# Second norm's transpositions placed at weight-tile boundaries of the out-projection, in a one-layer hybrid decoder trunk

## The chip, the core and the metric

The kernel runs on one core of a Trainium2 chip. The metric is the device time of one execution in microseconds (us); the median of several runs is compared. TensorE (PE) does the matrix work, VectorE (DVE), ScalarE (ACT) and GpSimd (POOL) the rest, SyncE (SP) issues most transfers.

## What is computed

One layer: RMSNorm, two token mixers merged by gates, an output projection added to the input, then a second RMSNorm and a squared-ReLU MLP added again, and a final norm. Sequence 1024, width 1024, MLP width 4096, float32. The part that matters here:

```
def rms_norm(x, gain):
    xf = x.astype(jnp.float32)
    y = xf * lax.rsqrt(jnp.mean(xf * xf, axis=-1, keepdims=True) + NORM_EPS)
    return (y * gain.astype(jnp.float32)).astype(x.dtype)
...
    y = jax.nn.sigmoid(m_a) * y_a + jax.nn.sigmoid(m_b) * y_b
    return y @ w_out
...
        h = rms_norm(x, norm_mix[l])
        x = x + hybrid_mixer(h, ...)
        h = rms_norm(x, norm_mlp[l])
        x = x + jnp.square(jax.nn.relu(h @ w_up[l])) @ w_down[l]
    return rms_norm(x, norm_final)
```

## The kernel before

**Matrix products.** Each float32 operand is split into a rounded high part and a rest (`split`: ACT casts the high part, DVE subtracts). `mm3` then issues three matmuls (lines 144, 145, 146 of the profile): high by high, high by rest, rest by high. Three matmuls of 128x512 into one PSUM bank are one step of a product.

**The out-projection, in two halves of 512 rows.** A row tile is 128 rows. `out_proj` does row tiles 0 to 3 of the sequence; its sums with the input land in `x2a`. The second half is written out in the loop over `part` (two parts of two row tiles each: 4 and 5, then 6 and 7) and `hf` (two halves of the 1024 output columns). Inside, `n` counts four steps, each with one weight tile `out_w[4 * hf + j]`, kept in SBUF: 2 k-slices x 2 row tiles x 3 matmuls = 12 matmuls. A part so has 96 matmuls. At the end of each `hf` DVE adds the sums to `x2s` (L1357). The last `hf` of part 1 takes its last two weight tiles first for one row tile, then for the other, so its `n` runs to 5.

**The second norm.** `second_norm(tt, half)` handles row tile `tt + 4 * half`. `norm_rows` squares and sums a row tile on ACT (L165), adds epsilon on DVE (L166), takes the power -0.5 on POOL (L171) and multiplies by it and the gain on DVE (L172, tile `xn_h`). Then eight 128x128 transpositions on TensorE (L1268) go into two banks of the PSUM tag "hg", which has two banks in all; ACT copies each bank back (L1269). For row tiles 0 to 3 the result is split at once into the operands B11 and B21. For 4 to 7 the generator `operands()` forms sums with row tile `tt` (t1, B22, n2, T3, T4: the operands of a seven-product Strassen scheme) and splits them.

**Behind it.** `product(q, step)` and `hidden(q, step)` are the up-projections of the MLP, by weight quads `q`. Three of their products (`uX` of quads 0 to 2) need only B11, one (`uZ`) B21; the others need the sums. `first_weights` and the calls after the loop prepare the split weights of quads 0 to 2 (`wA`, `ws10`, `ws30`, `wA120`) on ACT and DVE; they reuse SBUF tiles of weight tiles that the out-projection has finished with.

**What sets the order.** A scheduler orders each engine's instructions, within what the program pins. On TensorE `pin` keeps program order only while `pinned[0]` is true. Before the change this holds from `(part, hf) == (1, 1)` on; ahead of it the scheduler sets the transpositions of row tiles 0 to 5 among the matmuls of the parts. `keep` pins the norm's and the splits' operations on ACT and DVE.

Of the kernel before, what the change touches and what calls it, by code (L numbers as in the profile page):

```python
# [18 lines left out]
P = 128  # L19
# [26 lines left out]
def trunk(ctx: ExitStack, tc: tile.TileContext, x, wts, mlp, pv, gains, mask_f, mask_u, out):  # L46
    nc = tc.nc
    V, A, G, PE = nc.vector, nc.scalar, nc.gpsimd, nc.tensor
# [6 lines left out]
    def opened(name, **how):  # L55
        cm = tc.tile_pool(name=name, bufs=1, reuse_waits="tile", **how)
        return cm.__enter__(), lambda: cm.__exit__(None, None, None)
# [4 lines left out]
    def bank(tag, name):  # L62
        return ps.tile([P, 512], F32, tag=tag, name=name, bufs={"pj": 4, "sc": 2, "hg": 2}[tag])
# [3 lines left out]
    for i in range(NC * NPAIR):  # L67
        at = (0, 1, 2, 3, 4, 6, 5)
# [17 lines left out]
    def split(src, h, lo):  # L86
        keep(A.copy(h, src))  # L87
        ins = V.tensor_tensor(out=lo, in0=src, in1=h.bitcast(F32), op=ALU.subtract)  # L88
        keep(ins)
        return ins  # L90
# [45 lines left out]
    pinned = [False]  # L136

    def pin(ins):
        if pinned[0]:
            tc.keep_in_program_order(ins)  # L140

    def mm3(o, ah, al, bh, bl, first, last, goes_on=False):
        how = {"skip_group_check": True} if goes_on else {}
        pin(PE.matmul(o, ah, bh, start=first, stop=False, **how))  # L144
        pin(PE.matmul(o, ah, bl, start=False, stop=False, **how))  # L145
        pin(PE.matmul(o, al, bh, start=False, stop=last, **how))  # L146


    ident = const.tile([P, P], F32, tag="ident", name="ident")
# [668 lines left out]
    def stage(i):  # L818
        c, p = where(i)
        got = gots[i]  # L820
        if i == 0:
            yield from v_steps(c, p, got, lambda tt: None)
        elif i > 1:
            yield from v_of(i)

        def more(n):
            with tc.high_priority(400):
                transposed(xn1[n], hT[1], n, f"x1{n}")

        hooks = {at: lambda n=n: more(n) for at, n in {2: ((4, 1),), 3: ((2, 2), (6, 3))}.get(i, ())}  # L830
        px = yield from hooked(project_steps(c, f"xa{c}{p}"), hooks)
        xc, xps = conv_in(c, p, px)
        if i == 0:
            parameters()
            tc.keep_in_program_order(V.tensor_copy(mu, mu32.to_broadcast([P, 7, 8, 32])))
            pinned[0] = True
        yield
        if i == 1:
            gots[0]["tail"]()
            transposed(xn1[0], hT[1], 0, "x10")  # L840
        if i > 4:
            combos_on(2)

        def convolve():
            got["xc"] = conv(c, p, xc, xps, None)

        pq = yield from hooked(project_steps(c, f"q{c}{p}"), {} if i == 1 else {6: convolve})
        got["q1"] = q_of(c, p, pq)
        yield
        fs = hooked(project_steps(c, f"f{c}{p}"), {6: convolve} if i == 1 else {})  # L850
        for _ in range(5 if i != 1 else 7):
            next(fs)
            yield
        if i > 3:
            combos_on(1 if i == 4 else 2)
        if i == 1:
            pf = yield from fs
            got["f"], got["kk"] = f_of(c, p, pf)
            yield
        yield from rg_lru(c, p, got, *got["xc"])  # L860
        if i > 0:
            gots[i - 1]["normalised"]()
        for n in ((0,), (1,), (2, 3))[i] if i < 3 else ():
            xn1[n] = next_rows(n, gots[0]["states"] if i == 1 else None)
        if i != 1:
            pf = yield from fs
            got["f"], got["kk"] = f_of(c, p, pf)
# [74 lines left out]
    for i in range(NC * NPAIR):  # L942
        rest = stage(i + 1) if i + 1 < NC * NPAIR else last_stage()
# [238 lines left out]
    for q in own:  # L1182
        n = q + 1
# [60 lines left out]
    def homes(*names):  # L1244
        h2p.append(opened(f"h2{len(h2p)}", side="right"))
        for o in names:
            hop[o] = [h2p[-1][0].tile([P, 4, T], F32R, tag=o + q, name=f"h2{o}{q}") for q in ("H", "L")]
# [5 lines left out]
    def second_norm(tt, half):  # L1253
        cut = slice(tt * P, (tt + 1) * P)
        t = tt + 4 * half
        xs = x2s[tt] if half else x2a[tt]
        home = {3: "xn3", 4: "y01", 5: "y03", 6: "y00", 7: "y02"}.get(t, "xn")
        xn = n2p.tile([P, D], F32, tag=home, name=f"xn_h{t}", bufs=3 if home == "xn" else 1)
        norm_rows(xs, xn, gain1, f"h{t}")
        b = braw[tt, half] = xn.rearrange("p (h t) -> p h t", h=2)  # L1260

        def op_split(src, o):
            return split(src.rearrange("p (k t) -> p k t", k=4), hop[o][0][:, :, cut], hop[o][1][:, :, cut])

        for h in range(2):
            pt = bank("hg", f"xT_h{t}_{h}")
            for k in range(4):
                pin(PE.transpose(pt[:, k * P : (k + 1) * P], xn[:, (4 * h + k) * P : (4 * h + k + 1) * P], ident))  # L1268
            A.copy(b[:, h, :], pt)  # L1269
            if half == 0:  # L1270
                op_split(b[:, h, :], ("B11", "B21")[h])

        def operands():
            b0 = braw[tt, 0]
            b11, b21, b22, b12 = b0[:, 0, :], b0[:, 1, :], b[:, 1, :], b[:, 0, :]
            V.tensor_tensor(out=b11, in0=b11, in1=b12, op=ALU.subtract)
            t1_ops.append(op_split(b11, "t1"))
            yield
            for ins in (op_split(b22, "B22"), V.tensor_tensor(out=b12, in0=b22, in1=b12, op=ALU.subtract)):
                how = mybir.DependencyInfo(mybir.DependencyClass.NoSync, mybir.DependencyReason.DATA)  # L1280
                if tt > 1:
                    tc.add_manual_dep(ins.ins, t1_ops[-1].ins.name, how, reason="t1")
            V.scalar_tensor_tensor(b22, b11, -1.0, b22, op0=ALU.mult, op1=ALU.subtract)
            n2_ops.append(op_split(b22, "n2"))
            yield
            last = op_split(b12, "T3")
            if tt > 1:
                tc.add_manual_dep(last.ins, n2_ops[-1].ins.name, how, reason="n2")
            yield
            last = V.scalar_tensor_tensor(b21, b22, -1.0, b21, op0=ALU.mult, op1=ALU.subtract)  # L1290
            if tt > 1:
                tc.add_manual_dep(last.ins, n2_ops[-1].ins.name, how, reason="n2")
            op_split(b21, "T4")
            yield

        return operands()

    rest, t1_ops, n2_ops = [], [], []

# [26 lines left out]
                work[0]["sums"]()  # L1326
                work[0]["b"]()

    for tt in range(4):
        second_norm(tt, 0)  # L1330
    close_rows()
    homes("B22")
    for part in range(2):
        tts = (2 * part, 2 * part + 1)
        for tt in tts:
            x2s[tt] = n2p.tile([P, D], F32, tag="x2", name=f"x2s{tt}", bufs=2)
            nc.sync.dma_start(x2s[tt], x[(4 + tt) * P : (5 + tt) * P, :])
        for hf in range(2):
            pp = {tt: bank("pj", f"po1{hf}{tt}") for tt in tts}
            turn = [(j, tts) for j in range(4)]  # L1340
            if (part, hf) == (1, 1):
                turn = turn[:2] + [(j, tts[i : i + 1]) for i in range(2) for j in (2, 3)]
                pinned[0] = True
            for n, (j, those) in enumerate(turn):
                if n == 4:
                    first_weights()
                wh, wl = out_w[4 * hf + j]
                for k in range(2):
                    ku = 2 * j + k
                    yh, yl = ykt1(part, ku)  # L1350
                    cols = slice(k * 512, (k + 1) * 512)
                    for tt in those:
                        cut = slice((tt % 2) * P, (tt % 2 + 1) * P)
                        mm3(pp[tt], yh[:, cut], yl[:, cut], wh[:, cols], wl[:, cols], ku == 0, ku == 7)
            for tt in tts:
                cols = slice(hf * 512, (hf + 1) * 512)
                V.tensor_tensor(out=x2s[tt][:, cols], in0=pp[tt], in1=x2s[tt][:, cols], op=ALU.add)  # L1357
        for i, tt in enumerate(tts):
            if part:
                product(i, 0)  # L1360
            nc.sync.dma_start(x2d[4 + tt], x2s[tt])
            rest.append(second_norm(tt, 1))
    with tc.high_priority(400):
        work[0]["d"]()
    product(0, 3)
# [67 lines left out]
    for q in range(1, QUADS):  # L1433
        n = q + 1 if q + 1 < QUADS else QUADS + QUADS - 2
# [83 lines left out]
    for kb in range(n_kb):  # L1518
        last = kb + 1 == n_kb
        qs = order[2 * kb : 2 * kb + 2]  # L1520
        for half in range(2):
# [8 lines left out]
            for step, (bk, wo, uo), prs in [  # L1530
# [11 lines left out]
                for pr in prs:  # L1542
                    _, ci, cj, op = ADDS[step]
# [92 lines left out]
```

## Time and profile before

| | |
|---|---|
| runs, median (lowest to highest) | 1549.08 us (1548.0 to 1550.54), 3 runs |
| profiled execution: time, span | 1550.47 us, 1548.7 us |
| TensorE busy, matmuls | 1528.6 us, 9088 |
| DVE, ACT, POOL busy | 1151.0, 809.3, 154.5 us |
| mean granted TensorE clock | 0.999 |
| DMA | 306.82 MB, mean 198 GB/s |

The profile is of one execution; its times are us from the start of its span, the time from the first to the last instruction. In the timeline a row is: start, duration, engine, line, operation, output<-input, count, and in brackets the idle time of the engine ahead of it with what ended it. Matmuls are pipelined, so a row's duration is longer than the distance to the next row's start. A DVE or ACT row with "x2" holds two instructions back to back.

### The profile page before, as it was taken

The page shows a single profiled execution, that of the slowest core. Times are in us where ns is not written, and L with a number is a line of the kernel's source. Part 1 is how long each engine was busy: PE and PEld are TensorE (multiplying, and loading weights), DVE is VectorE, ACT ScalarE, POOL GpSimd, SP SyncE. Part 2 cuts the span into 40 slices and gives each one's busy share as a digit, 9 for nine tenths or more (in the row PEclk, how much of TensorE's full clock was granted, in tenths as well). Part 3 has the DMA queues.
Part 4 walks back from the last instruction along what each step waited for, and adds up shares of the span by engine and source line. Part 5 has one row for each costly group of instructions (what it writes and reads, how often), then busy time and mean ns, then how long its engine had stood idle before and what let it go on. Part 6 is the DMA issues. An engine that isn't in the chain of part 4 may idle for free. (4 is left out here: it accounts for less than half of the span.)

```text
span 1548.7 us, 23204 instructions
## 1 busy us (share of the span) xinstructions
PE 1528.6 (99%) x9088; PEld 1274.5 (82%) x9088; DVE 1151.0 (74%) x1656; ACT 809.3 (52%) x1341; POOL 154.5 (10%) x188
## 2 busy tenths in 40 slices
PE   9999999999999999999999999999999999999998
PEld 7878888888888887888888778888888788888886
DVE  5798695485675838786856568888888898888877
ACT  5656757567567335454533347766776721111115
POOL 1022210232614600000000000000000000000000
PEclk9999999999999999999999999999999999999999
DMA  8545455465674275332339223666666675666642
GB/s 295 191 158 191 150 192 195 150 215 173 222 229 140 99 295 187 126 136 82 136 107 333 117 109 141 268 246 250 248 251 247 220 307 215 253 250 251 253 187 109
DMA packets 81679, 306.82 MB, mean 198 GB/s; under 512 B 8481, under 2 KB 20897, under 8 KB 68642
## 3 DMA queue, kind: packets, MB, share of 16 engines
q1 hardware_dynamic: 77536, 292.75, 51.5%
q10 hardware_dynamic: 4034, 12.59, 2.1%
q8 instruction: 71, 1.16, 0.3%
q14 instruction: 38, 0.31, 0.1%
HBM read 201.50 MB, written 103.81 MB: 197 GB/s over the span
## 5 line engine op out<-in xcount | busy, mean ns | idle before, releaser
L1545 DVE TENSOR_TENSOR acc<-acc,dX 128x512 f32<-128x512 f32 x128 | 85.2, 685 | 28.8 <-PE dX L146 27.2
L87 ACT CAST wA<-q 128x512 fp32r<-128x512 f32 x46 | 28.6, 622 | 148.3 <-PE dX L146 102.4
L88 DVE TENSOR_TENSOR wL<-raw,wH 128x1024 fp32r<-128x1024 f32 x48 | 58.9, 1226 | 43.1 <-ACT wH L87 42.8
L87 ACT CAST wH<-raw 128x1024 fp32r<-128x1024 f32 x48 | 50.4, 1050 | 36.7 <-DMA raw<-wts_in 14.5
L1545 DVE TENSOR_TENSOR acc<-acc,dY 128x512 f32<-128x512 f32 x64 | 43.5, 686 | 13.1 <-PE dY L146 12.9
L145 PE MATMUL po<-wL,y 128*128 128x512 f32 x128 | 50.0, 391 | 0.0
L146 PE MATMUL po<-wH,y 128*128 128x512 f32 x128 | 49.9, 391 | 0.0
L144 PE MATMUL po<-wH,y 128*128 128x512 f32 x128 | 49.5, 390 | 0.0
L1406 ACT ACTIVATE b<-b 128x512 f32<-128x512 f32 x48 | 30.2, 630 | 32.7 <-DVE b L1405 32.5
L88 DVE TENSOR_TENSOR wA<-q,wA 128x512 fp32r<-128x512 f32 x46 | 31.5, 687 | 19.0 <-ACT wA L87 18.9
L108 ACT CAST wH<-raw 128x1024 fp32r<-128x1024 f32 x36 | 37.7, 1048 | 9.7 <-issue 3.7
L171 POOL TENSOR_TENSOR rstd_h<-rstd_h,mhalf 128x1 f32<-128x1 f32 x8 | 4.6, 585 | 376.1 <-DVE rstd_h L166 376.1
L465 DVE SCALAR_TENSOR_TENSOR xc<-xp,pvt,xc 128x512 f32<-128x512 f32 x48 | 40.1, 846 | 1.1 <-ACT xc L449 1.1
L981 DVE TENSOR_TENSOR s<-q,q 128x512 f32<-128x512 f32 x46 | 31.6, 688 | 5.3 <-DMA q<-mlp_in 5.0
L378 POOL TENSOR_TENSOR stt<-r,stt 128x256 fp32r<-128x256 f32 x16 | 19.8, 1261 | 127.4 <-ACT stt L377 115.3
L989 DVE TENSOR_TENSOR s<-q 128x512 f32<-128x512 f32 x46 | 31.6, 687 | 0.4
L1407 ACT ACTIVATE b<-b 128x512 f32<-128x512 f32 x48 | 30.2, 631 | 1.2
L769 ACT ACTIVATE on<-po 128x128 f32<-128x128 f32 x64 | 16.9, 278 | 26.1 <-PE po L765 26.0
L144 PEld LDWEIGHTS po<-wH,y 128*128 128x128 f32 x128 | 24.0, 188 | 4.9
L145 PEld LDWEIGHTS po<-wL,y 128*128 128x128 f32 x128 | 24.0, 188 | 4.9
L146 PEld LDWEIGHTS po<-wH,y 128*128 128x128 f32 x128 | 24.0, 188 | 4.8
L1071 DVE TENSOR_TENSOR gb<-gY,ge 128x512 f32<-128x512 f32 x14 | 9.7, 691 | 24.1 <-PE gY L146 24.1
(2548 smaller groups left out, 5453.6 us busy)
## 6 DMA issues: line engine op xcount, KB each, us to landing
q<-mlp_in SPq DMA_DIRECT2D x92, 512.0 KB, 3.7
raw<-wts_in SPq DMA_DIRECT2D x80, 512.0 KB, 4.8
rest<-wL SPq DMA_DIRECT2D x36, 512.0 KB, 2.9
wL<-rest SPq DMA_DIRECT2D x36, 512.0 KB, 4.1
hd<-ri SPq DMA_DIRECT2D x16, 256.0 KB, 3.8
od<-onT ACTq DMA_DIRECT2D x8, 512.0 KB, 7.1
cdT<-stT SPq DMA_DIRECT2D x16, 256.0 KB, 3.2
o<-od SPq DMA_DIRECT2D x4, 1024.0 KB, 7.4
```

The source lines that it names most:

```text
L87: keep(A.copy(h, src))
L88: ins = V.tensor_tensor(out=lo, in0=src, in1=h.bitcast(F32), op=ALU.subtract)
L108: A.copy(h, raw)
L144: pin(PE.matmul(o, ah, bh, start=first, stop=False, **how))
L145: pin(PE.matmul(o, ah, bl, start=False, stop=False, **how))
L146: pin(PE.matmul(o, al, bh, start=False, stop=last, **how))
L465: ins = V.scalar_tensor_tensor(xc[:, s, :], xp[:, j : j + T], pvt[:, PV_CW + 8 * j + u : PV_CW + 8 * j + u + 1], xc[:, s, :], op0=ALU.mult ...
L981: ins = V.tensor_tensor(out=sa[:, 0, :], in0=a21, in1=a22, op=ALU.add)
L989: V.tensor_tensor(out=sb[:, 0, :], in0=a21, in1=a11, op=ALU.add)
L1406: A.activation(b[:, at, :], b[:, at, :], AF.Relu, scale=-1.0 if at == 2 else 1.0)
L1407: A.activation(b[:, at, :], b[:, at, :], AF.Square)
L1545: V.tensor_tensor(out=dst, in0=dst, in1=banks[bk, pr], op=op)
```

## The change

`second_norm` no longer issues its transpositions, copies and B11/B21 splits itself. It returns them as a function `turned` beside the generator `operands()`. A dictionary `turns` holds these functions under a place `(part, hf, n)`: row tile 0 at (0, 0, 1), 1 at (0, 0, 2), 2 at (0, 0, 3), 3 at (0, 1, 0), 4 at (1, 0, 1), 5 at (1, 0, 2). After the matmuls of that weight tile the function is called. Row tiles 6 and 7 are turned at once as before. `pinned[0]` is set ahead of the loop, so TensorE's program order holds through both parts.

```diff
+        def turned():
+            for h in range(2):
+                pt = bank("hg", f"xT_h{t}_{h}")
+                for k in range(4):
+                    pin(PE.transpose(pt[:, k * P : (k + 1) * P], xn[:, (4 * h + k) * P : (4 * h + k + 1) * P], ident))
+                A.copy(b[:, h, :], pt)
+                if half == 0:
+                    op_split(b[:, h, :], ("B11", "B21")[h])
...
-        return operands()
+        return turned, operands()
...
-    for tt in range(4):
-        second_norm(tt, 0)
+    turns = {}
+    for tt, at in enumerate(((0, 0, 1), (0, 0, 2), (0, 0, 3), (0, 1, 0))):
+        turns[at], _ = second_norm(tt, 0)
     close_rows()
     homes("B22")
+    pinned[0] = True
...
             if (part, hf) == (1, 1):
                 turn = turn[:2] + [(j, tts[i : i + 1]) for i in range(2) for j in (2, 3)]
-                pinned[0] = True
...
+                if (part, hf, n) in turns:
+                    turns.pop((part, hf, n))()
...
-            rest.append(second_norm(tt, 1))
+            turn, ops = second_norm(tt, 1)
+            rest.append(ops)
+            if part:
+                turn()
+            else:
+                turns[1, 0, i + 1] = turn
```

TensorE at the start of part 0, before. Each "po" row is one matmul of the part into the bank of one of its two row tiles, "wH"/"wL" a weight tile's high part or rest; "xT_h" with "x4" are four transpositions into one "hg" bank:

```order
L144 MATMUL po_8539<-wH_8050,y_8150 128x512
L145 MATMUL po_8539<-wL_8051,y_8150 128x512
L1268 MATMUL xT_h_0_8446<-ident,xn_h_8440 128x128 x4
L1268 MATMUL xT_h_1_8454<-ident,xn_h_8440 128x128 x4
L146 MATMUL po_8539<-wH_8050,y_8150 128x512
L144 MATMUL po_8538<-wH_8096,y_8151 128x512
L145 MATMUL po_8538<-wL_8097,y_8151 128x512
L1268 MATMUL xT_h_0_8468<-ident,xn_h_8462 128x128 x4
L1268 MATMUL xT_h_1_8476<-ident,xn_h_8462 128x128 x4
L146 MATMUL po_8538<-wH_8096,y_8151 128x512
```

The first block stands behind 11 matmuls of the part, the second three matmuls later, each inside a group of three. The same engine and part after the change, around the first block:

```order
L144 MATMUL po_8475<-wH_8096,y_8151 128x512
L145 MATMUL po_8475<-wL_8097,y_8151 128x512
L146 MATMUL po_8475<-wH_8096,y_8151 128x512
L1269 MATMUL xT_h_0_8500<-ident,xn_h_8440 128x128 x4
L1269 MATMUL xT_h_1_8508<-ident,xn_h_8440 128x128 x4
L144 MATMUL po_8474<-wH_8102,y_8152 128x512
L145 MATMUL po_8474<-wL_8103,y_8152 128x512
```

The block now stands behind 24 matmuls, at the change from weight tile wH_8096 to wH_8102; the next three follow 12 matmuls apart. In part 1, before:

```order
L146 MATMUL po_8685<-wH_8050,y_8154 128x512
L144 MATMUL po_8684<-wH_8096,y_8155 128x512
L1268 MATMUL xT_h_0_8649<-ident,xn_h_8643 128x128 x4
L1268 MATMUL xT_h_1_8655<-ident,xn_h_8643 128x128 x4
L145 MATMUL po_8684<-wL_8097,y_8155 128x512
L146 MATMUL po_8684<-wH_8096,y_8155 128x512
L1268 MATMUL xT_h_0_8668<-ident,xn_h_8662 128x128 x4
L1268 MATMUL xT_h_1_8674<-ident,xn_h_8662 128x128 x4
L144 MATMUL po_8685<-wH_8096,y_8155 128x512
```

Row tile 4's block stood behind 13 matmuls of the part and row tile 5's behind 15; they move behind 24 and 36. On DVE, the same part from the norm of row tile 5 on, before ("ws10L", "wA120L", "ws30L": rests of split weights; L1276 and L1283: sums of row tiles; "s": sums of quad 1's raw weights "q"):

```order
L88 TENSOR_TENSOR ws10L<-s_8781,ws10H 128x1024
L1276 TENSOR_TENSOR xn_h_8440<-xn_h_8440,xn_h_8643 128x512
L1276 TENSOR_TENSOR xn_h_8462<-xn_h_8462,xn_h_8662 128x512
L88 TENSOR_TENSOR h2B22L<-xn_h_8643,h2B22H 128x4x128
L88 TENSOR_TENSOR h2t1L<-xn_h_8440,h2t1H 128x4x128
L88 TENSOR_TENSOR h2t1L<-xn_h_8462,h2t1H 128x4x128
L1279 TENSOR_TENSOR xn_h_8643<-xn_h_8643 128x512
L88 TENSOR_TENSOR wA120L<-q_8775,wA120H 128x1024
L1283 SCALAR_TENSOR_TENSOR xn_h_8643<-xn_h_8440,xn_h_8643 128x512
L981 TENSOR_TENSOR s_8897<-q_8791,q_8792 128x512
L88 TENSOR_TENSOR ws30L<-s_8782,ws30H 128x1024
L1357 TENSOR_TENSOR x2s_8680<-po_8684,x2s_8680 128x512
```

After:

```order
L88 TENSOR_TENSOR ws10L<-s_8781,ws10H 128x1024
L88 TENSOR_TENSOR wA120L<-q_8775,wA120H 128x1024
L1277 TENSOR_TENSOR xn_h_8440<-xn_h_8440,xn_h_8643 128x512
L88 TENSOR_TENSOR h2B22L<-xn_h_8643,h2B22H 128x4x128
L1280 TENSOR_TENSOR xn_h_8643<-xn_h_8643 128x512
L88 TENSOR_TENSOR h2t1L<-xn_h_8440,h2t1H 128x4x128
L1284 SCALAR_TENSOR_TENSOR xn_h_8643<-xn_h_8440,xn_h_8643 128x512
L88 TENSOR_TENSOR ws30L<-s_8782,ws30H 128x1024
L981 TENSOR_TENSOR s_8897<-q_8791,q_8792 128x512
L1361 TENSOR_TENSOR x2s_8656<-po_8660,x2s_8656 128x512
L988 TENSOR_TENSOR s_8897<-s_8897,q_8791 128x512
L1361 TENSOR_TENSOR x2s_8658<-po_8661,x2s_8658 128x512
```

Row tile 5's first sum, third here before, now comes only after these and two more rows; wA120L and the work of row tile 4 have moved ahead. From the add of row tile 6's second column half on, the order of every engine and of SyncE's queue is that of before.

More of the change, by code (lines that the diff above doesn't have):

```diff
@@ L1263, in op_split @@
             return split(src.rearrange("p (k t) -> p k t", k=4), hop[o][0][:, :, cut], hop[o][1][:, :, cut])
[L1265 to L1271, printed above, removed]
+        def turned():
[6 more added lines that the diff above has]
+                    op_split(b[:, h, :], ("B11", "B21")[h])
         def operands():
```

## Prediction

> **What bounds the kernel now.** I read the page's first part first, then the busy table of the two stretches in which the change lies, then TensorE's timeline there.
>
> ```profile
> PE 1528.6 (99%) x9088; PEld 1274.5 (82%) x9088; DVE 1151.0 (74%) x1656; ACT 809.3 (52%) x1341; POOL 154.5 (10%) x188
> ```
>
> TensorE is busy 99% of the span. The other engines have slack, so what lengthens or shortens TensorE's own stream sets the time; only some 20 of 1548.7 us are idle there at all. The next table has one row for each row part of the second out-projection (part 0, part 1): us, then each engine's busy time, then granted clock, DMA share and GB/s.
>
> ```profile
> 870.55:897.76 27.21, 25.96 (x129) 21.11 (x128) 12.95 (x21) 11.48 (x23) 2.16 (x4) 1.00 0.18 73
> 897.76:922.91 25.15, 23.93 (x113) 19.52 (x112) 18.89 (x29) 11.31 (x19) 1.34 (x3) 1.00 0.38 143
> ```
>
> TensorE lacks 1.25 us in part 0 and 1.22 us in part 1, at a granted clock of 1.00. DVE has much room in part 0 (12.95 of 27.21 us) and less in part 1 (18.89 of 25.15). What TensorE waits for is in the answer on the line of the transpositions:
>
> ```profile
> L1268 PE MATMUL xT_h<-ident,xn_h x64: 270/273/327, 873.5 to 930.2; 128*128 128x128 f32 x64
> its engine sat idle before it (us, times) until:
>   DVE xn_h L172: 0.9, 2
>   ACT ws10H L87: 0.7, 1
>   ACT h2B11H L87: 0.6, 1
>   DVE rstd_h L166: 0.3, 1
> ```
>
> So 2.5 us of idle stand before transpositions, in five of the eight blocks. A wait also empties the pipeline around it, so I price it by start times in TensorE's timeline. A block is eight transpositions; "po" rows are the matmuls of the parts.
>
> ```profile
> 870.55 0.39 PE L144 MATMUL po<-wH,y 128*128 128x512 f32 x1
> ...
> 877.22 0.39 PE L146 MATMUL po<-wH,y 128*128 128x512 f32 x1
> 877.45 1.03 PE L1268 MATMUL xT_h<-ident,xn_h 128*128 128x128 f32 x8
> ...
> 878.55 0.40 PE L145 MATMUL po<-wL,y 128*128 128x512 f32 x1
> ...
> 884.16 0.39 PE L144 MATMUL po<-wH,y 128*128 128x512 f32 x1
> ...
> 897.76 0.39 PE L144 MATMUL po<-wH,y 128*128 128x512 f32 x1
> ...
> 922.91 0.39 PE L144 MATMUL uX<-h2B11H,wA 128*128 128x512 f32 x1
> ...
> 925.41 0.40 PE L146 MATMUL uX<-h2B11H,wA 128*128 128x512 f32 x1
> ...
> 926.75 0.40 PE L145 MATMUL uX<-h2B11L,wA 128*128 128x512 f32 x1
> ```
>
> From 884.16 to 897.76 are the last 60 matmuls of part 0 with nothing between: 13.60 / 60 = 0.2267 us each. The block at 877.45 waited for nothing: from the matmul ahead of it to the second one behind it 1.33 us, less two steps of 0.2267, is 0.88 us. The block of row tile 6, which stands between the last two rows, gives 1.34 - 0.45 = 0.89. A free block costs 0.885 us.
>
> **The change, part by part.** No instruction is added or removed; the rows of every engine have the same count. Six of the eight blocks move on TensorE; the last two (row tiles 6 and 7) stay.
>
> *What the six cost now.* A part has 96 matmuls, 96 x 0.2267 = 21.76 us. Part 0 lasts 27.21 us, so its four blocks cost 5.45; part 1 lasts 25.15, so its two cost 3.39. Together 8.84 us. Six free blocks cost 6 x 0.885 = 5.31. What can go is 3.53 us: 1.91 in part 0, 1.62 in part 1.
>
> *Are the new places free?* The input of a block must be normalised (L172, on DVE) by then. First the line's answer for row tiles 0 to 3, then DVE's timeline for row tiles 4 and 5 with what follows:
>
> ```profile
> L172 DVE SCALAR_TENSOR_TENSOR xn_h<-x2a,rstd_h,gain x4: 1280/1284/1286, 872.2 to 878.6; 128x1024 f32<-128x1024 f32 x4
> ```
> ```profile
> 900.12 1.28 DVE L172 SCALAR_TENSOR_TENSOR xn_h<-x2s,rstd_h,gain 128x1024 f32<-128x1024 f32 x1 [0.72 <-POOL rstd_h L171]
> ...
> 902.19 1.28 DVE L172 SCALAR_TENSOR_TENSOR xn_h<-x2s,rstd_h,gain 128x1024 f32<-128x1024 f32 x1 [0.72 <-POOL rstd_h L171]
> 903.39 1.22 DVE L88 TENSOR_TENSOR ws10L<-s,ws10H 128x1024 fp32r<-128x1024 f32 x1
> 904.53 1.29 DVE L1276 TENSOR_TENSOR xn_h<-xn_h,xn_h 128x512 f32<-128x512 f32 x2
> ...
> 917.17 0.69 DVE L1290 SCALAR_TENSOR_TENSOR xn_h<-xn_h,xn_h 128x512 f32<-128x512 f32 x1
> 920.40 0.69 DVE L1357 TENSOR_TENSOR x2s<-po,x2s 128x512 f32<-128x512 f32 x1 [2.53 <-PE po L146]
> ```
>
> The first block now stands behind 24 matmuls: 870.55 + 24 x 0.2267 = 875.99, and its input is there at 872.2 + 1.28 = 873.5. The next follow every 12 matmuls and a block (3.61 us): 879.60, 883.21, 886.81. The last of the four inputs is there at 878.6 + 1.29 = 879.9, and each of the others at least 1.28 before the next, so row tile 1's by 877.4: all are early. Part 1 then starts at 895.85 instead of 897.76, and its norms, which hang on the end of part 0, move along by 1.91: row tile 4 is ready at 901.40 - 1.91 = 899.49 for a block at 895.85 + 24 x 0.2267 = 901.29, row tile 5 at 901.56 for a block at 904.90. The least margin is 1.8 us. Each block also takes both "hg" banks of the block before it, which ScalarE empties:
>
> ```profile
> 902.21 1.07 ACT L1269 COPY xn_h<-xT_h 128x512 f32<-128x512 f32 x2 [0.71 <-PE xT_h L1268]
> ```
>
> Both copies take 1.07 us; in part 1 one cast of about as much (wA120H, ws30H) now stands ahead of them. 3.6 us between blocks leave room for that; now the blocks stand 2 us apart.
>
> *What the later places cost.* Row tile 5 is turned at 904.90, now 903.62; measured from the start of part 1 that is 3.2 us later. DVE's queue is in a fixed order, and from ws10L on stand the same 21 operations before and after, up to the add of row tile 6's second column half (L1357, 920.40), only reordered. They run from 903.39 to 917.86 now, 14.47 us without a hole; then DVE idles 2.53 us. After the change they start at 901.48 and end at 915.95, and the add can come at 920.40 - 3.53 = 916.87. The cover shrinks from 2.5 to 0.9 us, but it holds, if nothing in the 21 waits. Row tile 5's first operation there is number 15, at about 911.7, some 4.5 us behind its copies (904.90, the block, one cast of ScalarE and 1.07: about 907). From that add on, all engines and SyncE's queue have the order of before, so the chain norm, transposition, t1, n2 of row tiles 6 and 7 starts 3.5 us earlier and ends 3.5 us earlier. TensorE waits once, and little, for its end:
>
> ```profile
> 939.12 0.50 PE L145 MATMUL uX<-h2n2L,ws10H 128*128 128x512 f32 x1 [0.17 <-DVE h2n2L L88]
> ```
>
> This wait stays as it is. Behind it nothing changes but the start, and TensorE bounds the rest.
>
> *A price that speaks against the change.* The eight transpositions of a free block take 0.88 us of TensorE's stream, though each lasts 0.273 us in its row: they overlap. The Trainium skill, page "TensorE: Matmul & The Clock Gate", section "Part 4: PE-mode transpose", puts a 128x128 transposition in a kernel's context at about 275 ns and says that it does not count as busy for the clock. Taken as what each takes from the stream, 48 of them would cost 13.2 us, more than the 8.84 measured, and nothing would be left to win. The trace agrees with the duration but not with that use of it, and its clock is 1.00 in both parts.
>
> **Sum.** The profiled execution took 1550.47 us (span 1548.7), the median of the three runs is 1549.08, so the execution that I read ran 1.4 us longer than the median; 3.5 us is far inside it and I subtract from the median: 1549.08 - 3.5 = 1545.6 us, 0.23% less. A measurement of this kernel can tell about 0.2%, 3.1 us, from no change.
>
> The unknown is a free block's price where it now stands, at a change of weight tile. Below, 0.85 is an estimate from the block at 877.45: seven of its eight starts' distances are (1.03 - 0.27) / 7 = 0.108, eight of these 0.87, and I go a little lower; the gain is then 3.7. Above, a block cannot take more than its whole length, 1.03 us, while nothing waits; six make 6.2, and the gain is 2.7. I take 0.885, because nothing is late at the new places.
>
> **The rivals.**
>
> *Part of it is lost* (17%). Blocks near 1.03 us, or DVE's remaining 0.9 us is used up by small waits among the 21 operations. Either leaves a gain of 1 to 3 us: 1546.1 to 1548.1. For it: 0.9 us is little. Against: each operation's source is ready well ahead by the sums above.
>
> *Absorbed later* (11%). Between the two MLP halves the chain of waits runs over a transfer:
>
> ```profile
> 1215.77 5.58 DMA q<-mlp_in
> ```
>
> Were that held by other traffic and not by its start, TensorE would come 3.5 us earlier and wait longer there: 1549.1. Against it: it starts when buffers come free, and those come free by work that moves along.
>
> *Each transposition takes its full length from TensorE* (2%): 48 x 0.273 = 13.1 us are more than the blocks cost now, no gain, 1549.1. This is the reading weighed above; a block of 0.88 us speaks against it.
>
> *Slower: DVE's queue stands on a load* (8%). L981 (sums of quad 1) is number 9 of the 21 and needs the quad's second half, loaded once ws10L has freed a buffer. First the time to landing of all such loads of the run, then the start of this one (and of the one behind it) on SyncE's timeline, then the slowest group of loads between 838 and 960 us:
>
> ```profile
> DMA to landing us min/median/max: 3.1/3.7/7.9
> ```
> ```profile
> 904.64 9.85 SPq L969 DMA_DIRECT2D q<-mlp_in  x2
> ```
> ```profile
> raw<-wts_in SPq DMA_DIRECT2D x3, 512.0 KB, 10.2
> ```
>
> The load now starts at 902.73. Eight operations are ahead of L981, three at 1.14 and five at 0.60 start to start, 6.4 us, so it is wanted at 907.9; at the median it lands at 906.4. It eats the gain only if it lands after 907.9 + 0.9 + 3.5 = 912.3, 9.6 us behind its start. At 12 us it would land at 914.7: 6.8 late, less 0.9 of cover, less 3.5, is 2.4 us slower, 1551.5. The longest of these loads took 7.9, and the group that took 10 was no such load; the DMA share of part 1 is 0.38.
>
> **Chances and range.** The forecast, a gain of over 3.1 us, has 62%. Faster is that case alone, 0.62; within 0.2% are the lost part, the later absorption and the full-length price, 0.17 + 0.11 + 0.02 = 0.30; slower is 0.08. The range runs from 1544.0 (gain 3.7, and the 1.4 us by which single executions stand off the median) to 1549.0, which takes in the lost part with some scatter and ends just short of the absorbed case: 0.62 + 0.17 = 0.79 lies inside.
>
> **What would show it.** Right: in the profile after, the stretch of part 0 lasts about 25.3 us, part 1 about 23.5, no idle before the six transposition blocks, the two last blocks as now, and DVE idle some 0.9 us before the add of row tile 6. Wrong in a step: blocks near or over 1 us at the new places (the price); DVE not idle before that add, or a longer wait at h2n2L or at the last two blocks (the cover); both parts short but the span not (absorbed later). An idle DVE before L981 with a load as its releaser would be the slower case.

## The result and the profile after

The change makes the kernel faster. The median of ten runs is 1546.25 us after (1544.07 to 1547.74) and 1550.3 us before (ten runs, 1548.0 to 1551.7). The ratio on record is 0.9977 with a 95% interval of 0.9969 to 0.9986 (the two medians alone would give 0.9974), so the gain is 0.23%, some 3.6 us, between 2.2 and 4.8. The forecast was 1545.6 us. The profiled execution took 1545.96 us with a span of 1544.2; the profiled execution before has a span of 1548.7.

The busy table of the page after:

```profile
PE 1527.4 (99%) x9088; PEld 1275.2 (83%) x9088; DVE 1150.1 (74%) x1656; ACT 809.7 (52%) x1341; POOL 153.7 (10%) x188
```

Nothing was added or removed: the counts are the same, and TensorE's busy time differs by 1.2 us. The busy table of the two stretches after (us, then the busy time of PE, PEld, DVE, ACT and POOL, the granted clock, DMA share and GB/s), and below them the stretch from the first uX matmul to the one that waits for h2n2L:

```profile
870.58:895.95 25.37, 25.37 (x129) 21.34 (x128) 12.95 (x21) 11.61 (x23) 2.15 (x4) 1.00 0.19 79
895.95:919.50 23.55, 23.55 (x114) 19.67 (x112) 18.75 (x29) 11.43 (x19) 1.35 (x3) 1.00 0.44 152
919.50:935.69 16.19, 15.99 (x78) 12.84 (x76) 14.99 (x24) 12.11 (x23) 1.13 (x2) 1.00 0.20 72
```

Part 0 lasts 25.37 us instead of 27.21, part 1 23.55 instead of 25.15, and in both TensorE is now busy for the whole stretch. Together that is 52.36 - 48.92 = 3.44 us. The third stretch was 16.21 us before (922.91 to 939.12) and is 16.19: what was won in the two parts is still there behind it. The line of the transpositions, after:

```profile
L1269 PE MATMUL xT_h<-ident,xn_h x64: 270/272/301, 876.0 to 926.8; 128*128 128x128 f32 x64
its engine sat idle before it (us, times) until:
```

The list of releasers under it is empty: no block waits any more. TensorE's timeline around the first moved block, row tile 5's block in part 1, and at the wait for h2n2L:

```profile
875.79 0.40 PE L146 MATMUL po<-wH,y 128*128 128x512 f32 x1
876.02 1.03 PE L1269 MATMUL xT_h<-ident,xn_h 128*128 128x128 f32 x8
876.81 0.48 PE L144 MATMUL po<-wH,y 128*128 128x512 f32 x1
877.13 0.40 PE L145 MATMUL po<-wL,y 128*128 128x512 f32 x1
...
904.78 0.39 PE L146 MATMUL po<-wH,y 128*128 128x512 f32 x1
905.01 1.03 PE L1269 MATMUL xT_h<-ident,xn_h 128*128 128x128 f32 x8
905.80 0.48 PE L144 MATMUL po<-wH,y 128*128 128x512 f32 x1
906.11 0.40 PE L145 MATMUL po<-wL,y 128*128 128x512 f32 x1
...
935.69 0.50 PE L145 MATMUL uX<-h2n2L,ws10H 128*128 128x512 f32 x1 [0.17 <-DVE h2n2L L88]
```

From the matmul ahead of the block to the second one behind it are 877.13 - 875.79 = 1.34 us, less two steps of 0.2267: a block costs 0.89 us at its new place, and row tile 5's (the second shown) 1.33 - 0.45 = 0.88. The wait for h2n2L is 0.17 us, as before. DVE's timeline after, at the sums of quad 1 and at the end of the work that moved:

```profile
907.99 0.68 DVE L981 TENSOR_TENSOR s<-q,q 128x512 f32<-128x512 f32 x1
...
914.60 1.28 DVE L1291 SCALAR_TENSOR_TENSOR xn_h<-xn_h,xn_h 128x512 f32<-128x512 f32 x2
916.98 0.69 DVE L1361 TENSOR_TENSOR x2s<-po,x2s 128x512 f32<-128x512 f32 x1 [1.09 <-PE po L146]
```

L981 starts without a wait, so the load of quad 1 is there in time. Before the add of row tile 6's second column half DVE is idle 1.09 us; before the change it was 2.53.

The spans differ by 4.5 us, more than the 3.44 of the stretch. The next table tells where the rest is. It has two profiled executions of each kernel; the starts are those of the first uX matmul, of the last matmul of the up-projection, and of the last matmul of the program.

| execution | first uX | last of up-projection | last matmul | first uX to last of up | from there to the last |
|---|---|---|---|---|---|
| before | 922.91 | 1235.21 | 1540.54 | 312.30 | 305.33 |
| before, again | 922.42 | 1233.67 | 1538.46 | 311.25 | 304.79 |
| after | 919.50 | 1231.02 | 1536.06 | 311.52 | 305.04 |
| after, again | 919.67 | 1231.66 | 1535.83 | 311.99 | 304.17 |

Behind the first uX, executions of one kernel differ by up to 1.1 us in a column, as much as the two kernels do. Over both columns they take 616.0 to 617.6 us, and the profiles of four kernels below whose stretch to the wait for h2n2L is 16.2 us too (places of before, one matmul later, part 0 alone, blocks twice) 615.8 to 618.9. What the first pair of profiles shows beyond 3.44 us lies inside this scatter; where it comes from is open.

### The profile page after: what moved, and what is told of

The parts are those of the page before. It is cut to its first block, busy times and chain, and to the rows that moved or that the text cites. A ratio compares the mean times of both kernels' runs of the same rounds, so it can differ in the third digit from the quotient of the medians.

```text
span 1544.2 us, 23204 instructions
## 1 busy us (share of the span) xinstructions
PE 1527.4 (99%) x9088; PEld 1275.2 (83%) x9088; DVE 1150.1 (74%) x1656; ACT 809.7 (52%) x1341; POOL 153.7 (10%) x188
## 5 line engine op out<-in xcount | busy, mean ns | idle before, releaser
L1554 DVE TENSOR_TENSOR acc<-acc,dY 128x512 f32<-128x512 f32 x64 | 43.4, 685 | 13.1 <-PE dY L146 12.9
L981 DVE TENSOR_TENSOR s<-q,q 128x512 f32<-128x512 f32 x46 | 31.6, 686 | 4.8 <-DMA q<-mlp_in 4.5
```

What stands on the lines that cost most here:

```text
L981: ins = V.tensor_tensor(out=sa[:, 0, :], in0=a21, in1=a22, op=ALU.add)
L1554: V.tensor_tensor(out=dst, in0=dst, in1=banks[bk, pr], op=op)
```

## Experiments

The theory: a moved block finds its input ready, so that it costs TensorE 0.88 us instead of up to 1.75; its exact place plays no part, and the work that DVE gets later is covered. The rivals: the gain is due to TensorE's kept order; or to the change of weight tile as a place; or a transposition takes its full length, so that the price is another; or DVE's cover is the edge. In all variants the places are written as counts of matmuls within a part:

```diff
-                        mm3(pp[tt], yh[:, cut], yl[:, cut], wh[:, cols], wl[:, cols], ku == 0, ku == 7)
-                if (part, hf, n) in turns:
-                    turns.pop((part, hf, n))()
+                        for m, (ya, wb) in enumerate(((yh, wh), (yh, wl), (yl, wh))):
+                            pin(PE.matmul(pp[tt], ya[:, cut], wb[:, cols], start=ku == 0 and m == 0, stop=ku == 7 and m == 2))
+                            count += 1
+                            if (part, count) in turns:
+                                turns.pop((part, count))()
```

The changed kernel's places are 24, 36, 48, 60 in part 0 and 24, 36 in part 1; the edits below are shown against the change written in this form. The comparisons with the kernel before are on one chip for each group of runs.

### Order written down, places of before

```diff
-    for tt, at in enumerate(((0, 24), (0, 36), (0, 48), (0, 60))):
+    for tt, at in enumerate(((0, 11), (0, 14), (0, 18), (0, 22))):
...
-                turns[1, (24, 36)[i]] = turn
+                turns[1, (13, 15)[i]] = turn
```

> TensorE's order pinned through both parts as after the change, but the six blocks pinned at the places where the scheduler had put them before (behind 11, 14, 18 and 22 matmuls of part 0, behind 13 and 15 of part 1). Theory (the gain is the waits in front of the blocks, gone because the blocks stand where their inputs are long ready): the waits are back; part 0 lasts 27.2 us, part 1 25.1, and the kernel takes the time of before, ratio 1.000. Rival (pinning TensorE's order is what gains): the time of after, ratio 0.9977.

Measured: 1548.06 us against 1549.19, ratio 0.9993 (0.9984 to 1.0001). This leaves out the rival's 0.9977. The stretch of the two parts:

```profile
870.58:922.08 51.50, 49.67 (x242) 40.65 (x241) 31.74 (x49) 22.70 (x42) 3.87 (x7) 1.00 0.29 108
```

That is 0.86 us less than the 52.36 of before, though TensorE's order is that of before. Part 1 lasts 25.15 us as expected, part 0 26.35 instead of the expected 27.2. The line's answer in this kernel, then DVE's, ScalarE's and TensorE's timelines at the fourth block:

```profile
L1269 PE MATMUL xT_h<-ident,xn_h x64: 270/272/329, 873.5 to 929.4; 128*128 128x128 f32 x64
its engine sat idle before it (us, times) until:
  DVE xn_h L172: 0.8, 2
  ACT ws10H L87: 0.7, 1
  DVE rstd_h L166: 0.3, 1
```
```profile
876.67 0.68 DVE L88 TENSOR_TENSOR h2B11L<-xn_h,h2B11H 128x512 fp32r<-128x512 f32 x1
877.78 1.28 DVE L172 SCALAR_TENSOR_TENSOR xn_h<-x2a,rstd_h,gain 128x1024 f32<-128x1024 f32 x1 [0.44 <-POOL rstd_h L171]
878.99 0.69 DVE L88 TENSOR_TENSOR h2B21L<-xn_h,h2B21H 128x512 fp32r<-128x512 f32 x1
```
```profile
879.26 0.65 ACT L87 CAST h2B11H<-xn_h 128x512 fp32r<-128x512 f32 x1
```
```profile
879.26 1.04 PE L1269 MATMUL xT_h<-ident,xn_h 128*128 128x128 f32 x8
```

One of five waits has gone, that of the fourth block. The same three engines at the same place before:

```profile
876.58 0.69 DVE L88 TENSOR_TENSOR h2B11L<-xn_h,h2B11H 128x512 fp32r<-128x512 f32 x1
877.18 0.69 DVE L88 TENSOR_TENSOR h2B21L<-xn_h,h2B21H 128x512 fp32r<-128x512 f32 x1
877.79 0.15 DVE L166 TENSOR_SCALAR rstd_h<-rstd_h 128x1 f32<-128x1 f32 x1
878.59 1.29 DVE L172 SCALAR_TENSOR_TENSOR xn_h<-x2a,rstd_h,gain 128x1024 f32<-128x1024 f32 x1 [0.66 <-POOL rstd_h L171]
```
```profile
879.24 0.65 ACT L87 CAST h2B11H<-xn_h 128x512 fp32r<-128x512 f32 x1
```
```profile
880.03 1.06 PE L1268 MATMUL xT_h<-ident,xn_h 128*128 128x128 f32 x8 [0.62 <-ACT h2B11H L87]
```

DVE's order is the only one that differs between the two, and there only in this: row tile 3's L166, which feeds its norm, stands ahead of row tile 0's two splits instead of behind them, and the norm itself (L172) ahead of the second. The norm starts 0.81 us earlier, and the fourth block 0.77. The wait before is put down to ScalarE's cast, whose end (879.89) came last by the profile, but it was not the cast: with the places pinned the same cast runs at the same time (879.26 to 879.91), and the block starts as it begins. What came earlier is the norm. Before, the block starts 0.15 us behind the norm's end (879.88), as the block of row tile 5 does (902.19 + 1.28 = 903.47, block at 903.62); now the norm ends 0.20 us ahead of the block, which waits for nothing. So writing the order down on TensorE brings nothing there; by way of DVE's order, which the scheduler makes anew, it brings 0.86 of the 3.44 us, at the fourth block.

### Later, but not at a change of weight tile

```diff
-    for tt, at in enumerate(((0, 24), (0, 36), (0, 48), (0, 60))):
+    for tt, at in enumerate(((0, 25), (0, 37), (0, 49), (0, 61))):
...
-                turns[1, (24, 36)[i]] = turn
+                turns[1, (25, 37)[i]] = turn
```

> The six blocks one matmul later than after the change, behind 25, 37, 49 and 61 matmuls of part 0 and 25 and 37 of part 1, so inside a group of three and inside a weight tile. Theory (being late enough is all): a block costs 0.885 us here too, part 0 lasts 25.3 us, part 1 23.5, ratio 0.9977. Rival (the change of weight tile is the better place, a block inside a group costs more): blocks at 1.1 us or more, parts 1.3 us longer in all or more, ratio 0.9985 or above.

Measured: 1546.16 us against 1549.19, ratio 0.9978 (0.9969 to 0.9987), and in the stretch:

```profile
870.47:919.39 48.92, 48.92 (x241) 41.01 (x240) 31.72 (x49) 23.06 (x42) 3.49 (x7) 1.00 0.31 114
```

48.92 us to the hundredth. The change of weight tile plays no part. What sets this kernel and the changed one apart from the one with the places of before is that the blocks stand late enough.

### Part 0 alone

```diff
-                turns[1, (24, 36)[i]] = turn
+                turns[1, (13, 15)[i]] = turn
```

> Only part 0's four blocks at the new places; part 1's two at their old ones, behind 13 and 15 matmuls. Theory: the two parts add up; part 0 lasts 25.3 us, part 1 25.1, the lead over the kernel before is 1.9 us when the up-projection starts and stays so, ratio 0.9988. Rival (only part 1's blocks count for the end, because the chain of waits behind it starts in part 1): ratio 1.000.

Measured: 1547.18 us against 1549.19, ratio 0.9987 (0.9978 to 0.9995), and in the stretch:

```profile
870.42:920.96 50.54, 49.33 (x241) 40.86 (x240) 31.86 (x49) 22.92 (x42) 3.49 (x7) 1.00 0.29 110
```

Part 0 gives 52.36 - 50.54 = 1.82 us, and what is still missing, 50.54 - 48.92 = 1.62, is part 1's share as worked out beforehand. The two parts add up.

### Each moved block twice

The eight transpositions of each of the six moved blocks are issued twice into the same bank; what is computed stays the same.

```diff
-                for k in range(4):
+                for k in list(range(4)) * (1 if t > 5 else 2):
```

> The places of after the change, and each of the six moved blocks issues its eight transpositions twice, into the same banks, so that the price of a block shows in the time. Theory (eight transpositions take 0.885 us from TensorE's stream): from the start of part 0 to the first up-projection matmul 48.9 + 6 x 0.87 = 54.2 us, 1.8 us above the kernel before, ratio 1.0010 to 1.0015. Rival (each takes its full 0.273 us): 48 x 0.273 = 13.1 us more, 62 us and ratio 1.006.

Measured: 1551.08 us against 1548.89, ratio 1.0012 (1.0003 to 1.0021). The stretch, and the first moved block in TensorE's timeline:

```profile
869.82:923.98 54.16, 54.16 (x289) 46.25 (x288) 32.35 (x49) 24.33 (x42) 3.50 (x7) 1.00 0.27 103
```
```profile
875.27 1.91 PE L1269 MATMUL xT_h<-ident,xn_h 128*128 128x128 f32 x16
```

48 more transpositions take 54.16 - 48.92 = 5.24 us, 0.873 for eight, 0.109 each, though each is listed at 272 ns. That transpositions take their full length from the stream is refuted: 48 of them would have taken 13.1 us. The whole time follows: from 0.9977 to 1.0012 (two comparisons, each with its interval above) are some 5.4 us.

### Row tile 5 later still

The cover of DVE was the weakest step. Row tile 5's block goes from behind 36 matmuls of part 1 to behind 72, and in further kernels to behind 81 and 84.

```diff
-                turns[1, (24, 36)[i]] = turn
+                turns[1, (24, 72)[i]] = turn
```

> As after the change, but row tile 5's block still later, behind 72 matmuls of part 1 instead of 36. Theory (the blocks may move later only as long as DVE's queue is through before the add of row tile 6; 0.9 us of cover are left): the block ends 18.1 us into part 1, its copies 19.2; five DVE operations of 0.60 stand behind them ahead of the add, which could start at 21.0 and now starts at about 22.3; the parts still last 25.3 and 23.5 us, but TensorE then waits for h2n2L 1.3 to 2 us longer, and of the 3.5 us some 1.5 to 2.2 are left: ratio 0.9987. Rival (DVE has slack behind the add as well, TensorE alone sets the time): ratio 0.9977, no longer wait at h2n2L.

Measured: 1546.07 us against 1549.19, ratio 0.9979 (0.9970 to 0.9988). DVE's timeline, TensorE's at row tile 7's block, and the stretch from the first uX to the wait for h2n2L:

```profile
914.12 0.69 DVE L1277 TENSOR_TENSOR xn_h<-xn_h,xn_h 128x512 f32<-128x512 f32 x1 [2.14 <-ACT xn_h L1270]
...
917.33 0.69 DVE L1364 TENSOR_TENSOR x2s<-po,x2s 128x512 f32<-128x512 f32 x1
```
```profile
926.38 1.06 PE L1269 MATMUL xT_h<-ident,xn_h 128*128 128x128 f32 x8 [0.69 <-ACT h2T4H L87]
```
```profile
919.20:935.87 16.67, 15.98 (x78) 12.84 (x76) 15.15 (x25) 12.56 (x25) 1.39 (x2) 1.00 0.22 86
```

DVE now waits 2.14 us for row tile 5, no idle is left before the add, and the add stands 1.87 us ahead of the first uX instead of 2.52: 0.65 late. Row tile 7's block waits 0.69, and the stretch grows by 0.48 us. The direction was expected, the size was not: the scheduler put one of the operations (L1291) behind the add, so that the add is less late than the sum of the moved work had it. The place was not expected either: no wait is listed at h2n2L in this profile, the lost time stands ahead of row tile 7's block. The whole time cannot tell, since its interval holds both the theory's 0.9987 and the rival's 0.9977; the stretch can.

```diff
-                turns[1, (24, 36)[i]] = turn
+                turns[1, (24, 84)[i]] = turn
```

> Row tile 5's block behind 84 of part 1's 96 matmuls. The scheduler then sets seven of DVE's operations on row tile 5 behind the add of row tile 6, where DVE idles 2.7 us in all ahead of h2n2L. Theory (the cover is bounded by DVE's queue up to h2n2L): the stretch to the first up-projection matmul stays 48.9 us, but from there to the first h2n2L matmul it is 17.5 to 18.5 us instead of 16.2; 1 to 2 us of the gain are left, ratio 0.9990. Rival (the place does not matter as long as it is late): 16.2 us, ratio 0.9978.

Measured: 1548.89 us against 1548.89, ratio 0.9999 (0.9990 to 1.0008): no gain is to be seen, where 0.9990 was expected. TensorE's timeline, then the busy table cut at what it shows:

```profile
936.61 0.50 PE L144 MATMUL uX<-h2n2H,ws10H 128*128 128x512 f32 x1 [2.29 <-ACT h2n2H L87]
...
938.66 0.63 PE L144 MATMUL uX<-h2n2H,ws10H 128*128 128x512 f32 x1
939.09 0.63 PE L145 MATMUL uX<-h2n2L,ws10H 128*128 128x512 f32 x1
```
```profile
936.60:938.66 2.06, 1.83 (x7) 1.23 (x7) 2.06 (x4) 0.00 (x0) 0.00 (x0) 0.98 0.00 0
938.66:942.04 3.38, 3.38 (x10) 2.63 (x9) 1.72 (x3) 1.63 (x3) 0.00 (x0) 0.51 0.00 0
942.04:946.00 3.96, 3.96 (x19) 3.27 (x18) 3.11 (x4) 2.27 (x6) 0.00 (x0) 1.00 0.40 121
```

TensorE waits 2.29 us for h2n2H, and from the first uX to the matmul on h2n2L 18.57 us (918.77 to 937.34) pass instead of 16.19. Two microseconds behind the wait the granted clock is 0.51 for 3.38 us: eight matmuls stand 0.43 us apart instead of 0.227, another 1.6 us. In this execution 3.44 - 2.4 - 1.6 leaves nothing of the gain. The wait alone would leave 1 us of it, ratio 0.9993, which the interval holds as well, so the whole time does not tell how many of the eleven runs had the slow stretch. Two more profiles were taken, of one execution each. The first is of this kernel again:

> The kernel with row tile 5's block behind 84 matmuls again, for a second profile. In the first one TensorE stood still for 2.3 us ahead of h2n2H, and 2 us later its granted clock was 0.51 for 3.4 us. Theory (the stall itself brings the slower clock): the stall is back, and a stretch at about 0.5 for about 3.4 us follows within a few us. Rival (the clock drop was an accident of that execution): the stall is back, the clock stays at 1.00.

It took 1550.73 us beside 1549.59 of one run of before. TensorE's timeline, with a wait in another place far behind, and its busy table over the matmuls behind the first of the two:

```profile
936.91 0.50 PE L144 MATMUL uX<-h2n2H,ws10H 128*128 128x512 f32 x1 [2.26 <-ACT h2n2H L87]
...
1148.25 0.50 PE L144 MATMUL uX<-h2T3H,ws311H 128*128 128x512 f32 x1 [1.81 <-ACT e L1414]
```
```profile
937.00:945.00 8.00, 7.78 (x33) 6.18 (x34) 6.79 (x10) 3.65 (x6) 0.00 (x0) 1.00 0.14 44
```

The wait is there again, and so are the 18.57 us, but the clock stays at 1.00. So such a wait does not always bring the half clock, and whether it brought it in the first execution is open. The second has the block behind 81 matmuls, `(24, 81)`:

> Row tile 5's block behind 81 matmuls of part 1. Theory (DVE's queue up to h2n2L is the cover, and it breaks little by little): between the kernel with 72 (0.5 us longer to the first h2n2L matmul) and that with 84 (2.4 us longer); TensorE stands still for 1 to 2 us ahead of h2n2, and as long as it is that short the granted clock stays at 1.00. Rival (any stall of over 1 us slows the clock): a stretch at about 0.5 behind it, and 1.6 us more lost.

It took 1547.5 us beside the same 1549.59, and the granted clock stays at 1.00. TensorE's timeline:

```profile
936.24 0.50 PE L144 MATMUL uX<-h2n2H,ws10H 128*128 128x512 f32 x1 [1.19 <-ACT h2n2H L87]
```

With row tile 5 behind 36, 72, 81 and 84 matmuls, the stretch from the first uX to h2n2L is 16.19, 16.67, 17.52 and 18.57 us. By the releasers shown, the chain through DVE and ScalarE is what the later places stand against, and it gives way by steps, far behind the place that the change takes.

### Both kernels once more

Before and after were each profiled once more without an edit, to see what of the difference behind the stretch comes back.

> The kernel before, unchanged, for a second profile. Theory (what the kernels differ by behind the first up-projection matmul is scatter between executions): 52.4 us from the start of part 0 to that matmul as in the first profile, and from it to the last up-projection matmul anything between 311.2 and 312.3 us, as in the kernels run so far. Rival (the change also saves some 0.7 to 1 us later, where the MLP halves meet): 312.3 us again, and 305.3 us from there to the last matmul.

> The kernel after, unchanged, for a second profile: 48.9 us from the start of part 0 to the first up-projection matmul. Behind it: theory (scatter), other times than the 311.5 and 305.0 us of the first profile by up to 1 us; rival (systematic), the same within 0.2 us.

They took 1548.39 and 1545.73 us; the stretch of before, then that of after:

```profile
870.10:922.42 52.32, 49.88 (x241) 40.62 (x240) 31.84 (x49) 22.80 (x42) 3.49 (x7) 1.00 0.28 107
```
```profile
870.75:919.67 48.92, 48.92 (x241) 41.01 (x240) 31.72 (x49) 23.04 (x42) 3.50 (x7) 1.00 0.31 114
```

The stretch repeats within 0.04 us, a difference of 3.40. The spans differ by 2.7 this time (1546.6 and 1543.9) and by 4.5 the first time: the two lie on both sides of the 3.4 us, as scatter behind the stretch would have it. The systematic rival's 312.3 and 305.3 us of before did not come back (311.25 and 304.79).

## Why the prediction was right

**The sum.** The prediction came out right in sign and size, by the mechanism that it gave: 1.91 and 1.62 us were worked out, 1.84 and 1.60 measured. The price of a block at its new place was taken as 0.885 and is 0.88 to 0.89; repeating the blocks gave 0.873 by another way. Neither bound (0.85, 1.03) was needed. The forecast time is 0.65 us under the measured 1546.25, and the three runs that it starts from have a median 1.2 us under that of the ten; it is the difference that came out, more than the time.

**New places ready.** Shown by the empty list of releasers. The reason "nothing is late at the new places" is the right one: one matmul past the change of weight tile the stretch is the same.

**The cover.** 0.9 us of idle were worked out before the add of row tile 6, 1.09 measured. The 21 operations run without a hole. The wait for h2n2L stayed at 0.17 and the stretch to it kept its length.

**The rivals.** Nothing was lost in part: the whole time, a gain of 2.2 to 4.8 us, could not rule out the upper end of the 1 to 3 us of that rival, but the stretch does, with 3.44 and 3.40. Nothing was absorbed later as far as the runs can tell: the whole times follow the stretches, 3.44 us less with ratios 0.9977 and 0.9978, 1.82 less with 0.9987, 1.80 more (blocks twice) with 1.0012. The full-length price of a transposition falls with the doubled blocks. DVE did not stand on the load at L981; its start was worked out as 907.9 and is 907.99.

**What the prediction did not see.** It put all 3.53 us down to the new places. A quarter, 0.86 us, comes already with the rewriting, without a block moved, because the scheduler puts the norm of row tile 3 on DVE ahead of a split that went before it. The sum is the same, since a block that has its input early costs 0.885 either way. And the margin of 0.9 us, called little, was not an edge: row tile 5 behind 72 matmuls used it up and lost only 0.48 us; behind 84 it lost 2.4, and in one of two executions a stretch of half clock followed.

## What to carry to other kernels

Price a group of instructions that stands in a full stream by start times, from the neighbour ahead to the second one behind, less the neighbours' own step; idle time and listed length were both wrong prices here (2.5 us of idle were listed where 3.44 were won, and 8 x 0.27 us for a block that takes 0.88). Move work on the bounding engine to any place where its input has long been ready and no tidy boundary is needed, and then follow the engines that get their work later up to the first wait that they set. Where a scheduler orders the other engines, compare their order with the order of the edit that moves nothing: part of a gain may be theirs.

## What the runs showed of the hardware

A wait of TensorE in a full stream costs more than its listed idle time. Priced by start times, the five blocks that waited in the kernel before cost 1.40, 1.40, 1.71, 1.75 and 1.62 us, with 0.30, 0.32, 0.62, 0.68 and 0.54 us of idle listed ahead of them; over the 0.885 of a free block that is the idle time and each time some 0.2 us more. Five times 0.2 is the difference between the 2.5 us listed and the 3.44 won.

A slow clock followed one long wait and not another. In one of two executions with a wait of 2.3 us, the granted clock was 0.51 for 3.38 us, two microseconds after the wait had ended, which took another 1.6 us. Up to its last matmul, none of the twelve profiles shows another stretch under 1.00, though they have waits of 1.2 to 1.8 us as well. That the wait brought the slow stretch is not shown. The Trainium skill, page "TensorE: Matmul & The Clock Gate", section "Why this matters for your kernels", advises against idle gaps of more than about 3 us between bursts of matmuls, and its section "What's actually happening" has the clock fall to a half after an idle window of about 3.4 us that runs free of the program. The half clock and the length of the slow stretch agree with that page of the Trainium skill. The gap does not: it was 2.3 us of idle, 2.68 from start to start, less than both figures, and in the other execution no slow stretch stands behind a gap as long. What made the difference between the two executions is open.
